# Other weight slots for V, a weighted k without GpSimd, and w_mo loaded within the first tile of an mLSTM core

## The chip, the cores and the metric

The kernel runs on one core of one Trainium2 chip. The metric is the device time of one execution in microseconds (us). A core has five engines: TensorE (PE in the profile; its weight loads are PEld), VectorE (DVE), ScalarE (ACT), GpSimd (POOL) and SyncE (SP), whose queue issues nearly all transfers between DRAM and the on-chip memory SBUF. Matmul results land in PSUM. Each engine works through its own queue in order and waits on semaphores for the others.

## The reference

Two sequences (2048 and 256 tokens, 1024 wide) go through two layers and a final norm:

```python
xn = rms_norm(x, norm_g[0]); x = x + window_attention_mixer(xn, ...)   # 16 heads, 4 KV heads, window 128
xn = rms_norm(x, norm_g[1]); x = x + mlstm_mixer(xn, ...)              # 4 heads, both directions
y  = rms_norm(x, final_norm_g)
```

The change lies in the second layer. It projects `xn` to q, k (512 each), v, o, z (1024 each) and 16 gates. For each head and direction, running over chunks s of the sequence, with weights w made of the gates:

```python
C_loc = einsum('bhcsk,bhcsv->bhckv', w[..., None] * kc, vc)   # state of one chunk
C_new = sp * C + sl * C_loc                                   # carried on
num   = P @ vc + sc * (qc @ C)                                # P: decay times q k^T
h     = num / max(|den|, exp(-m))
```

The two directions are added, normalized, multiplied by `sigmoid(o) * silu(z)` and projected by `w_out` (in the kernel `w_mo`).

## The kernel before

The 2304 tokens are 18 tiles of 128 (`NT`); the kernel takes 128 tokens as one chunk. Every fp32 product is made of three matmuls on parts: a value is split into `hi` (a cast to fp32r) and `lo` (the rest), and hi*hi, lo*hi and hi*lo are added. So each weight block of 128 x 512 that is loaded costs a transfer into a raw buffer, a cast on ACT and a subtraction on DVE. `stage` (line 109) takes the next raw buffer of a ring and issues the transfer on SP (line 113); the ring `raww` has eight buffers (`NRW`).

The parts go into **slots**. `self.free` is a queue of 29: `y0` to `y7`, `w0` to `w15`, `x0` to `x4`, in three pools. `slot` (line 130) takes the first one, `release` (line 179) puts the taken ones back in front, in the order in which they were taken. A slot that is taken again can be written only when the last matmul that read it is done.

The stages in order, each of them a method:

- attention: `attn_core`, `attn_gate`, `attn_out`.
- `mlstm_qkv` (line 640): q and k by `winograd_pass` (line 337), over pairs of tiles. It loads 16 quarter blocks (`quarters`, line 200, the parts by `part`, line 184, with the cast at line 189 and the subtraction at line 190). The first pair is multiplied plainly (`plain`, line 314), and meanwhile `combinations` (line 212) makes the Strassen-Winograd sums `t2`, `t3`, `t1`, `t4` of the quarters (subtractions at lines 218, 226). The other pairs use seven products in the order `b11`, `t2`, `b21`, `t3`, `t1`, `t4`, `b22` (`winograd`, line 277; its half products are lines 273 to 275). 28 slots are in use then, and are released in that order.
- V in the same method: `load_w` (line 138; cast at line 165 or, with a scale, 167; subtraction at line 169 or 171) fills 24 slots with the V columns of `w_qkvg`: eight for the first block of 512, then eight times two for blocks of 272 and 256. Then each tile is projected (`project`, line 371).
- `gate_sums` (line 686): small operations that make the gates' sums and maxima. The scan over the tiles is lines 742 and 745, about 70 operations on DVE; the exponentials on ACT are lines 749, 756, 769, 776.
- `mlstm_gates_states` (line 814): two Winograd passes over `w_oz` (sigmoid at line 851, products at lines 853 and 858, the result `go` stored at line 859) and, between the pairs, the states of the backward direction. `weighted_k` (line 790) makes w*k for one tile: a multiplication on POOL (line 796), a cast on ACT (797), a subtraction on DVE (798), each over all four heads at once. Here it is called with d=1 and a ring of three raw buffers, `rawk`.
- `mlstm_core` (line 865): per tile, four generators: `weights(t+1)` makes the decay matrices and loads the next tile's operands (E at line 887; products at lines 904 to 911), `core(t)` computes the heads, `update(t)` the forward state (it calls `weighted_k` with d=0, and raw buffers of `raww`), `back(t-1)` projects by `w_mo`. The string `ORDER` says how their steps are interleaved. `w_mo`, 16 blocks, is loaded after `weights(0)` and ahead of that loop, into the 16 `w` slots, which the last pass over `w_oz` still uses. `update(t)` runs for all tiles but the last of each sequence, 16 of 18.

The order on each engine isn't the program's order alone. The kernel is built with a scheduler that simulates the engines with estimated times and lays out each queue: what is ready first goes first, and of what is ready, what stands earlier in the program. So work is taken up as early as its buffers are free, sometimes stages ahead, but the order is fixed before the kernel runs.

Of the kernel before, what the change touches and what calls it, by code (L numbers as in the profile page):

```python
# [11 lines left out]
F32 = mybir.dt.float32  # L12
F32R = mybir.dt.float32r
BF16 = mybir.dt.bfloat16
AF = mybir.ActivationFunctionType
ALU = mybir.AluOpType
# [11 lines left out]
MH, DQK, DV = 4, 128, 256  # L28
# [17 lines left out]
AORDER = "fffssssfsffffppsvppv"  # L46
AORDER1 = "fffssssfsffffppsvppv"
AORDER2 = "ssppsspvpv"
KX, WL = 0, 0
PH3, PL3 = (), ()  # L50
EA, ES, EQ = 2, 18, 0
ORDER = "cubwbubccucbcbuwubbbbbbw"
# [3 lines left out]
def seg_of(t):  # L56
    for s in SEGS:
        if s[0] <= t < s[1]:
            return s


class Trunk:
# [577 lines left out]
    def mlstm_qkv(self, first):  # L640
        nc, tc, a = self.nc, self.tc, self.a
        with ExitStack() as st:
            p = st.enter_context(tc.tile_pool(name="b1", bufs=2, reuse_waits="tile"))
            ps = st.enter_context(tc.tile_pool(name="b1ps", bufs=1, space=PSUM, reuse_waits="tile"))
            nc.sync.dma_start(self.gbias, a["gbias"].to_broadcast([128, 16]))

            def use(t, b, o, u):
                y = p.tile([128, MH, DQK], F32, tag="qk"[b], name="qk"[b], bufs=2)
                yf = y[:].rearrange("p h d -> p (h d)")
                if u is None:  # L650
                    nc.scalar.copy(yf, o)
                else:
                    nc.vector.tensor_add(yf, o, u)
                if b:
                    nc.scalar.mul(yf, yf, DQK ** -0.5)
                    nc.sync.dma_start(self.k[t][:], y[:])
                tp = ps.tile([128, MH, 128], F32, tag="tr", name="tr", bufs=1)
                for h in range(MH):
                    nc.tensor.transpose(tp[:, h, :], y[:, h, :], self.ident[:])
                yT = p.tile([128, MH, 128], F32, tag="yT", name="yT", bufs=2)  # L660
                (nc.vector.tensor_copy if b else nc.scalar.copy)(yT[:], tp[:])
                nc.sync.dma_start((self.kT if b else self.qT)[t][:], yT[:])

            self.winograd_pass(self.xn2T, a["w_qkvg"], 0, None, use, first=first)


            w = self.load_w(a["w_qkvg"][:, 1024:], [[512], [272, 256]])
            self.release()
            for t in range(NT):
                xs = self.load_x(self.xn2T[t])  # L670
                v = p.tile([128, MH, VW], F32, tag="v", name="v", bufs=2)
                nc.gpsimd.memset(v[:, :, DV:], 1.0)
                for b in range(3):
                    pj = self.pj()
                    self.project(pj, xs, w[b])
                    if b == 0:
                        nc.scalar.copy(v[:, 1:3, :DV], pj[:].rearrange("p (h d) -> p h d", h=2))
                    elif b == 1:
                        nc.vector.tensor_copy(v[:, 0, :DV], pj[:, :DV])
                        nc.vector.tensor_add(self.gates[:, t, :], pj[:, DV:DV + 16], self.gbias)  # L680
                    else:
                        nc.vector.tensor_copy(v[:, 3, :DV], pj[:, :DV])
                nc.sync.dma_start(self.v[t][:], v[:])
# [106 lines left out]
    def weighted_k(self, p, t, d, raw=()):  # L790

        nc = self.nc
        k = self.stage(self.k[t][:].rearrange("p h d -> p (h d)"), *raw).rearrange("p (h d) -> p h d", h=MH)
        lo = p.tile([128, MH, DQK], F32R, tag="kl", name="kl", bufs=1)
        hi = p.tile([128, MH, DQK], F32R, tag="kh", name="kh", bufs=1)
        nc.gpsimd.tensor_mul(k, k, self.w[:, d, t, :].unsqueeze(2).to_broadcast([128, MH, DQK]))
        nc.scalar.copy(hi[:], k)
        nc.vector.tensor_sub(lo[:], k, hi[:].bitcast(F32))
        return hi, lo
# [65 lines left out]
    def mlstm_core(self, y):  # L865
        nc, tc, a = self.nc, self.tc, self.a
        with ExitStack() as st:
            pool = lambda n, **k: st.enter_context(tc.tile_pool(name=n, bufs=2, reuse_waits="tile", **k))
            TRP, TRT = self.sps, "s"
            py, pv, pm, p, pe = pool("b3y", side="right"), pool("b3v"), pool("b3m"), pool("b3"), self.early  # L870
            ps = pool("b3ps", space=PSUM)
            cm = self.cm
            w = []
            fg = pm.tile([128, D], F32, tag="fg", name="fg", bufs=1)
            nc.sync.dma_start(fg[:], a["final_g"].to_broadcast([128, D]))
            state = {0: None}
# [71 lines left out]
            def update(t):  # L948
                s0, s1 = seg_of(t)
                if t == s1 - 1:  # L950
                    state[t + 1] = None
                    return
                kw = self.weighted_k(pv, t, 0, () if t < KX else ("raww",))
                yield
                C = p.tile([128, MH, VW], F32, tag="C", name="C", bufs=2)
                state[t + 1] = C
                for h in range(MH):
                    self.state_update(ps, 0, t, kw, W[t][3], state[t], C, t == s0, [h], 1)
                    yield

            def back(t):
                hh = H[t][:].rearrange("p h d -> p (h d)")
                xs = []
                for b in range(2):
                    tp = TRP.tile([128, 4, 128], F32, tag=TRT, name="tr", bufs=1)
                    for j in range(4):
                        nc.tensor.transpose(tp[:, j, :], hh[:, (b * 4 + j) * 128:(b * 4 + j + 1) * 128], self.ident[:])
                    xs += self.split(tp[:].rearrange("p c q -> p (c q)"))
                    yield
                x = [p.tile([128, 512], F32, tag="x", name="x", bufs=3)[:] for b in range(2)]  # L970
                for b in range(2):
                    nc.sync.dma_start(x[b], self.x2[t][:, b * 512:(b + 1) * 512])
                for b in range(2):
                    po = self.pj()
                    for qt in range(4):
                        self.project(po, xs, w[b], range(qt * 2, qt * 2 + 2))
                        if qt == 3:
                            nc.vector.tensor_add(x[b], x[b], po[:])
                        yield
                rs = p.tile([128, 1], F32, tag="rs", name="rs", bufs=2)  # L980
                self.rms(p, x, rs[:])
                for b in range(2):
                    cols = slice(b * 512, (b + 1) * 512)
                    nc.vector.scalar_tensor_tensor(x[b], x[b], rs[:], fg[:, cols], ALU.mult, ALU.mult)
                    nc.sync.dma_start(y[t * 128:(t + 1) * 128, cols], x[b])
                yield

            self.free = deque(x for x in self.free if x[0] is self.wp)
            for _ in weights(0):
                pass  # L990
            if not WL:
                w += self.load_w(a["w_mo"], [[512]] * 2, self.g[:, 2], PH3, PL3)
            for t in range(NT + 1):
                gens = {"c": core(t) if t < NT else iter(()), "u": update(t) if t < NT else iter(()),
                        "b": back(t - 1) if t > 0 else iter(()), "w": weights(t + 1) if t + 1 < NT else iter(())}
                for i, k in enumerate(ORDER):
                    if t == 0 and i == WL and WL:
                        w += self.load_w(a["w_mo"], [[512]] * 2, self.g[:, 2], PH3, PL3)
                    next(gens[k], None)
                for g in gens.values():  # L1000
                    for _ in g:
                        pass
# [111 lines left out]
```

## Time and profile before

| | |
|---|---|
| median of three runs | 2317.96 us (2316.12 to 2319.85) |
| profiled execution | 2321.67 us, its span 2319.6 us |
| granted clock of TensorE | 0.98 of full speed on average |
| busy in the span | PE 96%, PEld 76%, DVE 67%, ACT 47%, POOL 20% |

In the stage views each row is a stretch of the span: its limits, its length, then the busy time of PE, PEld, DVE, ACT and POOL with the number of instructions in brackets, the granted clock, the busy share of the DMA engines and GB/s. In a timeline a row is a start, a duration, the engine, the line, the operation, what it writes and reads, and in square brackets how long the engine was idle before and what ended that. "x3" merges three operations that follow each other. In a group the last column is idle time of the engine before these instructions. `ACTq` or `SPq` is the sequencer of an engine.

### The profile page before, as it was taken

How to read it: one execution, taken by the hardware profiler on the slowest of the kernel's cores; microseconds unless marked ns; L12 is line 12 of the kernel's file. 1: busy time of each engine (PE TensorE's matmuls, PEld its weight loads, DVE VectorE, ACT ScalarE, POOL GpSimd, SP SyncE). 2: the span in 40 equal slices, each digit the busy share in tenths (PEclk: the TensorE clock that was granted, in tenths of full speed). 3: DMA queues.
4: the chain of work that ended last, by engine and by line, in shares of the span. 5: the costliest groups of instructions: out<-in, count | busy, mean ns of one | idle time of the engine just before them, and what ended most of it. 6: DMA issues, size and time to landing. Idle time of an engine off the chain costs nothing.

```text
span 2319.6 us, 32951 instructions
## 1 busy us (share of the span) xinstructions
PE 2225.3 (96%) x11102; PEld 1769.0 (76%) x11102; DVE 1549.3 (67%) x3403; ACT 1089.6 (47%) x2500; POOL 456.4 (20%) x392
## 2 busy tenths in 40 slices
PE   8999999999999999999999999969999996999998
PEld 7766666666667887888788899858887885888887
DVE  7565656565877779778656311577698676777784
ACT  6454545454764335445434211454353444554453
POOL 3211111111102221322000000012232216333320
PEclk9999999999999999999999999979999997999999
DMA  7111111111215457667534522443465357655551
GB/s 264 48 38 48 38 48 38 48 41 37 95 53 198 156 166 235 215 204 235 190 121 164 171 97 95 158 160 120 146 211 184 117 186 252 215 191 202 207 164 69
DMA packets 170281, 326.41 MB, mean 141 GB/s; under 512 B 18784, under 2 KB 21632, under 8 KB 170112
## 3 DMA queue, kind: packets, MB, share of 16 engines
q1 hardware_dynamic: 169968, 324.30, 41.8%
q8 instruction: 88, 1.44, 0.3%
q14 instruction: 81, 0.66, 0.1%
q10 hardware_dynamic: 144, 0.01, 0.0%
HBM read 235.34 MB, written 88.89 MB: 140 GB/s over the span
## 4 chain that ended last, share of the span: by engine, by line
PE 71%; DVE 12%; DMA 7%; ACT 6%; issue 3%; POOL 1%; SPq 0%; DVEq 0%; POOLq 0%; ACTq 0%
PE pj L377 8%; PE pj L379 8%; PE pj L378 8%; PE pj L273 4%; PE pj L275 4%; PE pj L274 4%; PE ptp L528 3%; PE o L540 3%; PE c L274 3%; PE c L273 3%; PE c L275 3%; PE d L273 3%; PE d L274 3%; PE d L275 3%; DMA qs<-rows 2%
## 5 line engine op out<-in xcount | busy, mean ns | idle before, releaser
L122 ACT CAST xhi<-rawx 128x512 fp32r<-128x512 f32 x372 | 228.5, 619 | 475.8 <-PE pj L378 106.8
L377 PE MATMUL pj<-whi,xhi 128*128 128x512 f32 (+2 forms) x1152 | 433.2, 377 | 10.1 <-ACT whi L167 5.6
L379 PE MATMUL pj<-whi,xlo 128*128 128x512 f32 (+2 forms) x1152 | 422.6, 372 | 5.2 <-DVE xlo L123 5.2
L378 PE MATMUL pj<-wlo,xhi 128*128 128x512 f32 (+2 forms) x1152 | 425.7, 370 | 0.0
L123 DVE TENSOR_TENSOR xlo<-rawx,xhi 128x512 fp32r<-128x512 f32 x338 | 241.9, 720 | 77.5 <-ACT xhi L122 71.1
L377 PEld LDWEIGHTS pj<-whi,xhi 128*128 128x128 f32 x1152 | 217.5, 189 | 52.1 <-issue 8.8
L379 PEld LDWEIGHTS pj<-whi,xlo 128*128 128x128 f32 x1152 | 217.5, 189 | 49.8 <-DVE xlo L123 9.4
L378 PEld LDWEIGHTS pj<-wlo,xhi 128*128 128x128 f32 x1152 | 217.4, 189 | 36.2 <-issue 2.4
L515 ACT ACTIVATE Sm<-Sm,nm 128x384 f32<-128x384 f32 (+1 forms) x288 | 167.1, 582 | 94.8 <-DVE nm L509 88.4
L273 PE MATMUL pj<-whi,xhi 128*128 128x512 f32 x480 | 196.0, 409 | 5.2 <-ACT xhi L122 1.7
L274 PE MATMUL pj<-wlo,xhi 128*128 128x512 f32 x480 | 194.2, 405 | 1.7 <-DVE wlo L190 1.7
L275 PE MATMUL pj<-whi,xlo 128*128 128x512 f32 x480 | 192.9, 403 | 0.0
L504 DVE CUSTOM_DVE_ANT_0 Sm<-s,mask 128x384 f32<-128x384 f32 (+1 forms) x272 | 136.0, 529 | 71.0 <-PE s L502 67.9
L528 PE MATMUL ptp<-ident,Sm 128*128 128x128 f32 x800 | 135.7, 282 | 8.3 <-DVE PT L531 5.1
L528 PEld LDWEIGHTS ptp<-ident,Sm 128*128 128x128 f32 x800 | 95.6, 142 | 52.2 <-ACT Sm L515 18.0
L274 PE MATMUL d<-wlo,xhi 128*128 128x512 f32 x320 | 126.7, 396 | 1.3 <-DVE wlo L190 1.3
L273 PE MATMUL c<-whi,xhi 128*128 128x512 f32 x320 | 127.6, 399 | 0.0
L274 PE MATMUL c<-wlo,xhi 128*128 128x512 f32 x320 | 127.4, 398 | 0.0
L275 PE MATMUL c<-whi,xlo 128*128 128x512 f32 x320 | 127.2, 398 | 0.0
L273 PE MATMUL d<-whi,xhi 128*128 128x512 f32 x320 | 127.1, 397 | 0.0
L275 PE MATMUL d<-whi,xlo 128*128 128x512 f32 x320 | 126.8, 396 | 0.0
L189 ACT CAST whi<-raww 128x512 fp32r<-128x512 f32 x144 | 86.1, 618 | 76.6 <-DVE raww L218 25.2
(241 smaller groups left out, 4678.8 us busy)
## 6 DMA issues: line engine op xcount, KB each, us to landing
rawx<-xn2T SPq DMA_DIRECT2D x144, 256.0 KB, 3.1
x<-x SPq DMA_DIRECT2D x108, 256.0 KB, 3.9
rawx<-xT SPq DMA_DIRECT2D x72, 256.0 KB, 2.9
raww<-w_oz SPq DMA_DIRECT2D x64, 256.0 KB, 4.3
raww<-w_qkvg SPq DMA_DIRECT2D x40, 256.0 KB, 3.5
v<-v SPq DMA_DIRECT2D x18, 516.0 KB, 3.7
rawx<-v SPq DMA_DIRECT2D x36, 258.0 KB, 2.8
rawx<-x SPq DMA_DIRECT2D x36, 256.0 KB, 3.0
```

The lines of the kernel that those rows point to most:

```text
L122: nc.scalar.copy(hi[:], src)
L123: (eng or nc.vector).tensor_sub(lo[:], src, hi[:].bitcast(F32))
L189: nc.scalar.copy(hi[:], raw)
L273: nc.tensor.matmul(o, xh, wh, start=i == 0 and not more, stop=False, skip_group_check=more)
L274: nc.tensor.matmul(o, xh, wl, start=False, stop=False, skip_group_check=more)
L275: nc.tensor.matmul(o, xl, wh, start=False, stop=i == 3, skip_group_check=more)
L377: nc.tensor.matmul(o[:, :n], xh, wh, start=kt == 0, stop=False)
L378: nc.tensor.matmul(o[:, :n], xh, wl, start=False, stop=False)
L379: nc.tensor.matmul(o[:, :n], xl, wh, start=False, stop=kt == KT - 1)
L504: nc.vector.tensor_tensor_reduce(Sm[:, :nk], S[:, :nk], mask[:, t % 3, win, :], 1.0, MASKED, ALU.add, ALU.max, mx[:, c:c + 1])
L515: nc.scalar.activation(Sg[c][:, :nk], Sg[c][:, :nk], AF.Exp, bias=nm[:, c:c + 1], scale=HD ** -0.5, accum_out=rs[:, c:c + 1])
L528: nc.tensor.transpose(tp[:, c, :], Ss[g][c][:, j, :], self.ident[:])
```

## The change

Three edits. In `mlstm_qkv`, before V's weights are loaded, the queue of free slots is turned so that the slot that the pass over q and k left unused comes first, the five next (the first ones released) are set aside, and V takes the other 24. Afterwards the five come to the front, followed by the others of their pool, so that the pass over `w_oz` takes these first. In `weighted_k`, for d=0 only, the multiplication on POOL is left out: per head, ACT makes `hi` as k times the weight, and DVE makes `lo` as k times the weight less `hi`. Its raw buffers in the core are two that are taken off the ring `raww`, which keeps six. And `w_mo` is loaded inside the loop, at step 12 of the 24 of tile 0, instead of ahead of it.

```diff
-KX, WL = 0, 0
+WL = 12
@@ mlstm_qkv
             self.winograd_pass(self.xn2T, a["w_qkvg"], 0, None, use, first=first)
+            self.free.rotate(1)
+            last = self.free.popleft()
+            kept = [self.free.popleft() for _ in range(5)]
+            self.free.appendleft(last)
             w = self.load_w(a["w_qkvg"][:, 1024:], [[512], [272, 256]])
             self.release()
+            first = [x for x in self.free if x[0] is kept[0][0]]
+            self.free = deque(kept + first + [x for x in self.free if x not in first])
@@ weighted_k
+        if d == 0:
+            for h in range(MH):
+                wk = self.w[:, d, t, h:h + 1]
+                nc.scalar.activation(hi[:, h], k[:, h], AF.Copy, scale=wk)
+                nc.vector.scalar_tensor_tensor(lo[:, h], k[:, h], wk, hi[:, h].bitcast(F32), ALU.mult, ALU.subtract)
+            return hi, lo
         nc.gpsimd.tensor_mul(k, k, self.w[:, d, t, :].unsqueeze(2).to_broadcast([128, MH, DQK]))
         nc.scalar.copy(hi[:], k)
         nc.vector.tensor_sub(lo[:], k, hi[:].bitcast(F32))
@@ mlstm_core
             w = []
+            ring = self.rings["raww"]
+            self.rings["rawk"] = deque(ring.pop() for _ in range(2))
@@ update
-                kw = self.weighted_k(pv, t, 0, () if t < KX else ("raww",))
+                kw = self.weighted_k(pv, t, 0, ("rawk",))
@@ the loop of mlstm_core
-            if not WL:
-                w += self.load_w(a["w_mo"], [[512]] * 2, self.g[:, 2], PH3, PL3)
             for t in range(NT + 1):
...
                 for i, k in enumerate(ORDER):
-                    if t == 0 and i == WL and WL:
+                    if t == 0 and i == WL:
                         w += self.load_w(a["w_mo"], [[512]] * 2, self.g[:, 2], PH3, PL3)
```

## The prediction

> **What bounds the kernel now.** I read the page's busy times first, then the busy times by stage, then the timelines of the stages that the diff touches.
>
> ```profile
> span 2319.6 us, 32951 instructions
> PE 2225.3 (96%) x11102; PEld 1769.0 (76%) x11102; DVE 1549.3 (67%) x3403; ACT 1089.6 (47%) x2500; POOL 456.4 (20%) x392
> ```
>
> TensorE (PE) is busy 96% of the span, so only the 94.3 us in which it stands still, or runs at a low clock, can be won. The next view gives the stages (us; busy time of PE, PEld, DVE, ACT, POOL with instruction counts; granted clock; DMA share; GB/s).
>
> ```profile
> 1255.00:1285.00 30.00, 30.00 (x141) 24.46 (x140) 22.64 (x43) 18.39 (x40) 0.00 (x0) 1.00 0.79 263
> 1440.00:1480.00 40.00, 40.00 (x263) 36.67 (x262) 8.96 (x20) 6.69 (x11) 0.32 (x3) 1.00 0.21 73
> 1491.60:1528.00 36.40, 25.34 (x122) 20.30 (x120) 33.01 (x72) 20.31 (x33) 0.00 (x0) 0.90 0.76 253
> 1528.00:1542.60 14.60, 5.07 (x19) 3.98 (x19) 9.76 (x74) 5.19 (x11) 1.83 (x2) 0.50 0.22 72
> 1911.80:1953.00 41.20, 20.72 (x89) 16.43 (x87) 27.81 (x52) 20.36 (x51) 28.18 (x23) 0.67 0.85 298
> 1953.00:2300.00 347.00, 341.76 (x1884) 293.56 (x1884) 256.57 (x643) 178.27 (x502) 106.19 (x95) 1.00 0.54 180
> ```
>
> V's start (1255 to 1285) and V itself have PE full. Two holes remain beside the diff: the gate sums after V (1491.6 to 1542.6, PE idle 11.1 + 9.5 = 20.6 us) and the start of the core (1911.8 to 1953, idle 20.5 us). The core's later tiles lose 5.2 us in 347. So the forecast is about those two holes.
>
> In the first hole the chain of waits and the timelines show what ends it.
>
> ```profile
> 1515.47 1.05 PE L897 MATMUL s<-qT,kT 128*128 128x128 f32 x8
> ...
> 1542.62 0.79 PE L273 MATMUL pj<-whi,xhi 128*128 128x512 f32 x1 [1.61 <-DVE e L853]
> ```
>
> ```profile
> 1533.89 0.32 ACT L749 ACTIVATE spr<-spr 1x144 f32<-1x144 f32 x1 [7.72 <-DVE spr L748]
> ...
> 1541.25 1.08 ACT L851 ACTIVATE e<-pj 128x512 f32<-128x512 f32 x2
> ```
>
> PE waits for a PSUM buffer that the sigmoid of line 851 has to read; on ACT that sigmoid stands behind the exponentials of the gate sums, and the first of these waits 7.72 us for DVE. DVE is 33.01 of 36.4 us busy until 1528, then runs the scan alone. So DVE's load ahead of the scan sets when PE goes on.
>
> **The change part by part. 1: other slots for V.** Followed through the queue of free slots by hand: before, V takes the slots y0 to y7 for its first block, and the first eight of the 16 quarter blocks of w_oz need just those, so their casts wait for V's last tile. After, V takes x4 (unused until now), y5 to y7, and slots of `b21`, `t3`, `t1`, `t4` and `b22`; y0 to y4 stay free.
>
> ```profile
> L113 SPq DMA_DIRECT2D raww<-w_oz x8: 328/382/390, 1274.8 to 1284.1; - x8
> ```
>
> ```profile
> 1481.48 4.82 ACT L189 CAST whi<-raww 128x512 fp32r<-128x512 f32 x7 [0.20 <-PE pj L379]
> ```
>
> ```profile
> 1482.32 4.70 DVE L190 TENSOR_TENSOR wlo<-raww,whi 128x512 fp32r<-128x512 f32 x7
> ```
>
> ```profile
> 1483.04 11.91 SPq L113 DMA_DIRECT2D raww<-w_oz  x14
> ```
>
> The loads are issued as early as their raw buffers allow (1274.8), 200 us before their casts. With five slots free I expect five casts and five subtractions to go up into V's stage, where DVE has 31 of 40 us free, and five of the 14 loads now issued from 1483 on to follow them. The hole then loses 5 x 4.70/7 = 3.4 us of DVE work, and perhaps DVE's waits for those loads:
>
> ```profile
> L190 DVE TENSOR_TENSOR wlo<-raww,whi 128x512 fp32r<-128x512 f32 x32 | 21.2, 684 | 1.6 <-ACT whi L189 1.6
> L226 DVE TENSOR_TENSOR raww<-raww 128x512 f32<-128x512 f32 x4 | 2.7, 685 | 2.8 <-DMA raww<-w_oz 2.8
> ```
>
> 2.8 us at line 226. Both ends: -6.2 us, and +2 us if the queue of DVE is laid out anew with the gate steps later (three 0.67 us operations put ahead of them; no row excludes it). I take **-4.5**: all of the work, and 1.1 of the 2.8, since most loads stay. The half clock after the pause (0.50 until 1542.6) stays, because 16 us of pause remain.
>
> ```profile
> 1953.54 0.23 PE pj L378
> ```
>
> The price is at V's start: the last four blocks of V's weights now wait for `b22`, which the last pair of q and k uses last. PE has no idle time there (30.00 of 30.00), and behind that product lie V's first block and six of eight steps of its second as other work: 24 matmuls at 0.23 us (a step of the chain, from a later stage) are 5.6 us, against a cast and a subtraction of 4.82/7 + 4.70/7 = 1.4 us for the first. I take 0; with that cover gone it is +2.8 us for four narrower blocks of half that cost each.
>
> **2: weighted k without GpSimd (POOL).** Per tile this removes one multiplication on POOL, one 512-wide cast on ACT and one 512-wide subtraction on DVE; it adds four 128-wide scaled copies on ACT and four fused operations on DVE.
>
> ```profile
> L796 POOL TENSOR_TENSOR raww<-raww,scr x16: 1034/1038/1484, 1918.9 to 2080.6; 128x512 f32<-128x512 f32 x16
> L798 DVE TENSOR_TENSOR kl<-raww,kh x16: 679/1255/1840, 1922.5 to 2245.0; 128x512 fp32r<-128x512 f32 x16
> L797 ACT CAST kh<-raww x16: 602/610/631, 1920.4 to 2244.4; 128x512 fp32r<-128x512 f32 x16
> L906 ACT ACTIVATE E<-E,scr x144: 384/390/405, 1545.6 to 2248.4; 128x128 f32<-128x128 f32 x144
> L931 DVE SCALAR_TENSOR_TENSOR r<-num,scr x72: 143/150/160, 1923.1 to 2288.0; 128x2 f32<-128x2 f32 x72
> L935 DVE SCALAR_TENSOR_TENSOR hh<-num,r,hh x72: 470/480/486, 1927.6 to 2290.9; 128x256 f32<-128x256 f32 x72
> ```
>
> ACT: 4 x 0.39 for 0.61, at most +0.95 us a tile. DVE: a fused operation of width 128 lies between 0.15 (width 2) and 0.48 (width 256); halfway, 0.31, gives 1.26 for four, against 0.68 undisturbed and 1.26 in the median. In the later tiles this lies under PE (DVE 74%, ACT 51% busy of 347 us), and I cost it at nothing; with the cover gone it is 16 x 0.58 = 9.3 us.
>
> [...]
>
> **3: k's own two buffers, and w_mo later.** This is about the second hole, on SP's queue and POOL:
>
> ```profile
> 1920.92 2.00 SPq L113 DMA_DIRECT2D raww<-k  x2
> 1923.22 0.32 SPq L859 DMA_DIRECT2D go<-e  x1
> ```
>
> ```profile
> 1918.86 1.48 POOL L796 TENSOR_TENSOR raww<-raww,scr 128x512 f32<-128x512 f32 x1
> 1920.31 1.72 POOL L858 TENSOR_TENSOR e<-e 128x512 f32<-128x512 f32 x1
> ...
> 1925.48 8.02 POOL L796 TENSOR_TENSOR raww<-raww,scr 128x512 f32<-128x512 f32 x8
> ```
>
> ```profile
> 1918.93 0.63 ACT L851 ACTIVATE e<-s 128x512 f32<-128x512 f32 x1 [1.07 <-POOL e L858]
> ```
>
> ```profile
> go<-e SPq DMA_DIRECT2D x36, 256.0 KB, 3.2
> ```
>
> ```profile
> 1923.22 5.17 DMA go<-e
> ...
> 1929.78 5.74 DMA E<-rows
> ...
> 1935.55 1.04 DVE E L904
> ```
>
> With eight raw buffers k is loaded many tiles ahead, just where the last gate product `go` has to be stored; its store is ahead of E of tile 1 on SP's queue, and E starts the chain to 1953. Without line 796 the last `e` is ready at 1918.93 + 0.63 + 1.72 = 1921.3 instead of 1922.0, and without the two k loads its store is issued then, not at 1923.22: -1.9 us. The store takes 5.17 us against a median of 3.2; six fewer k loads (256 KB each, 1.6 MB) and two more of w_mo (its ring has six buffers now) leave 1.05 MB less to move, 3.5 us at the stage's 298 GB/s, if all of that were waited for. Against it stands k's cast on the same chain, +0.6 to +1.2. Ends: -1.9 - 3.5 = -5.4, and +1.2 without any gain; I take **-3.0**.
>
> All 16 loads of w_mo, with 16 ACT and 16 DVE operations, are moved behind half of tile 0 in the program. In the trace before:
>
> ```profile
> 1914.65 7.92 DVE L171 SCALAR_TENSOR_TENSOR wlo<-raww,g,whi 128x512 fp32r<-128x512 f32 x5
> ```
>
> ```profile
> 1953.04 0.50 PE L377 MATMUL pj<-whi,xhi 128*128 128x512 f32 x1 [0.57 <-ACT xhi L122]
> ```
>
> they end at 1922.6 and are first read at 1953.04: 30 us of slack, so I cost the move at nothing.
>
> Sum: -4.5 - 3.0 + 0 = -7.5 us. The profiled execution took 2321.67 us (span 2319.6 and 2.1 around it), 3.7 over the median of 2317.96; I subtract from the median: **2310.5 us**.
>
> **The rivals.** *Only one hole shrinks* (the gate chain keeps its place among DVE's work, or E's load still waits): -3 to -4.5, about 2314. For it: both are orders laid out from estimated times. *Nothing changes*, 2318: the five casts aren't taken up into V, because the free slots are no use while the raw buffers hold others; the eight early loads at 1274.8 speak against it. *w_mo comes late* (the slower one): casts left over at 1922.6 run into the chain of 1935 to 1953.
>
> ```profile
> 1920.00:1930.00 10.00, 4.20 (x13) 3.29 (x14) 4.58 (x11) 6.68 (x18) 9.37 (x9) 0.50 0.76 277
> 1930.00:1940.00 10.00, 3.73 (x24) 3.00 (x22) 4.19 (x12) 4.14 (x14) 6.00 (x6) 0.84 1.02 346
> 1940.00:1953.00 13.00, 9.48 (x36) 8.01 (x36) 10.84 (x22) 4.05 (x11) 7.16 (x6) 0.57 0.69 239
> ```
>
> DVE has 5.4 + 5.8 + 2.2 = 13.4 us free there, room for eight casts at the 7.92/5 = 1.58 us just shown. From the ninth on each costs 1.58; all 16 cost 12, less 4.5 from the first hole: +7.5, 2325.5. *POOL's relief helps the core*: of its 106 us of POOL work 16 x 1.04 = 16.6 go, and DVE's 1.26 against 0.68 at line 798 tells of disturbance. Then the core's 5.2 us of PE idle time go too: -12.7, 2305. [...]
>
> **How the numbers follow.** Forecast 0.48; one hole 0.20; nothing 0.12; w_mo late 0.13; POOL's relief 0.07. A measurement of this kernel can't tell less than about 0.2%, 4.6 us, from no change. Faster: most of the forecast (0.43), the relief (0.07), a third of one hole (0.07): 0.57. Slower: w_mo late and a little of nothing: 0.15. Same: 0.28. The forecast's own ends are -6.2 - 5.4 = -11.6 and about -3; with the relief -16.8, 2301, and with a small loss 2321. Outside lies most of w_mo late and little else.
>
> **What would show it.** Five of line 189's casts between 1285 and 1480, and 27 instead of 32 of line 190 in the first hole; the scan (lines 742, 745) starting some 4 us sooner after V's last tile; no run of k loads ahead of the last `go` store, E of tile 1 landing about 3 us sooner; line 171 ended before DVE starts on E. I am wrong if V's start gets PE idle time, if casts of line 171 stand between E's arrival and the first line 377, or if the scan starts as late as before.

## The result, and the profile after

The changed kernel takes 2322.18 us (median of 13 runs, 2320.42 to 2324.25); the kernel before, run beside it, 2316.77 us (13 runs, 2311.99 to 2319.85). The ratio is 1.0026, 95% interval 1.0017 to 1.0035: slower by 4 to 8 us, where 7.5 us less had been forecast. The time lies just above the forecast's range, which ended at 2321.

The page of the changed kernel (span; busy time of each engine, share of the span, instructions):

```profile
span 2321.4 us, 33033 instructions
PE 2221.7 (96%) x11102; PEld 1763.0 (76%) x11102; DVE 1548.0 (67%) x3451; ACT 1099.5 (47%) x2548; POOL 436.8 (19%) x376
```

The profiled execution took 2323.22 us, 1.0 over its median, while that of before stood 4.9 over its own. So spans can't be set against each other directly. Five events that both programs have cut the execution into stretches. First their rows in the timeline of the changed kernel (start, duration, engine, line, operation; in brackets the idle time before it and what ended that): a step of the normalization on POOL, V's last matmul, the first product that the hole of the gate sums holds up, and the first projection of the core.

```profile
1041.42 0.55 POOL L391 TENSOR_TENSOR rs<-ss,epst 128x1 f32<-128x1 f32 x1 [6.12 <-DVE ss L390]
...
1497.85 0.28 PE L379 MATMUL pj<-whi,xlo 128*128 128x256 f32 x1
...
1546.29 0.79 PE L273 MATMUL pj<-whi,xhi 128*128 128x512 f32 x1 [1.61 <-DVE e L865]
...
1949.85 0.50 PE L377 MATMUL pj<-whi,xhi 128*128 128x512 f32 x1 [0.68 <-ACT xhi L122]
```

The first two in the timeline of the kernel before (the other two, at 1542.62 and 1953.04, stand in the prediction), with its two copies of q, which matter below:

```profile
1044.12 0.55 POOL L391 TENSOR_TENSOR rs<-ss,epst 128x1 f32<-128x1 f32 x1 [6.23 <-DVE ss L390]
...
1098.57 0.56 ACT L651 COPY q<-pj 128x512 f32<-128x512 f32 x1
...
1102.61 0.57 ACT L651 COPY q<-pj 128x512 f32<-128x512 f32 x1
...
1492.09 0.28 PE L379 MATMUL pj<-whi,xlo 128*128 128x256 f32 x1
```

Before, this first event is 2.7 us later, in a part of the program that the change doesn't touch; a stretch that begins there is free of that. The lengths in us:

| | to V's last matmul | the hole | to the first projection | to the end | all four |
|---|---|---|---|---|---|
| before | 448.3 | 50.3 | 410.4 | 366.6 | 1275.5 |
| after | 456.7 | 48.2 | 403.6 | 371.6 | 1280.0 |
| difference | +8.5 | -2.1 | -6.9 | +5.0 | +4.5 |

So the second half wins 4.0 us, and everything is lost ahead of V's end, where nothing had been forecast. The stages of the changed kernel (limits, length, busy time of PE, PEld, DVE, ACT, POOL, granted clock, DMA share, GB/s):

```profile
1044.00:1145.00 101.00, 94.36 (x432) 76.83 (x431) 78.30 (x135) 54.21 (x103) 14.71 (x13) 0.97 0.69 226
1115.00:1120.00 5.00, 5.00 (x14) 3.85 (x14) 3.56 (x12) 3.55 (x7) 0.00 (x0) 0.59 0.92 279
1276.00:1300.00 24.00, 21.67 (x119) 18.36 (x118) 15.56 (x33) 12.81 (x29) 0.00 (x0) 1.00 0.84 286
1498.10:1546.30 48.20, 29.67 (x135) 23.47 (x133) 40.55 (x142) 23.55 (x40) 1.64 (x2) 0.78 0.59 190
1908.80:1949.80 41.00, 24.62 (x115) 19.27 (x113) 31.94 (x61) 25.25 (x62) 14.75 (x11) 0.83 0.84 298
1949.80:2321.40 371.60, 354.84 (x1939) 303.23 (x1939) 270.29 (x701) 190.91 (x553) 100.34 (x92) 0.99 0.54 177
```

The same view of the kernel before, where the prediction doesn't have it:

```profile
1044.00:1145.00 101.00, 99.20 (x459) 80.41 (x458) 80.16 (x137) 56.94 (x110) 15.08 (x12) 0.98 0.69 226
1276.00:1300.00 24.00, 24.00 (x139) 20.79 (x138) 13.01 (x27) 9.73 (x21) 0.00 (x0) 1.00 0.79 268
1953.00:2319.60 366.60, 353.64 (x1936) 302.92 (x1936) 262.92 (x655) 181.51 (x510) 107.31 (x97) 1.00 0.52 174
```

PE stands still for 6.6 us in 1044 to 1145 (before 1.8) and 2.3 us at V's start (before nothing). The 6.6 us are one wait. In the timeline of the changed kernel the transposes of q (line 659) wait for the copies of q on ACT (line 651):

```profile
1112.20 0.62 ACT L165 CAST whi<-raww 128x512 fp32r<-128x512 f32 x1 [1.74 <-DMA raww<-w_qkvg]
...
1113.24 1.06 ACT L651 COPY q<-pj 128x512 f32<-128x512 f32 x2
...
1113.88 1.11 PE L659 MATMUL tr<-ident,q 128*128 128x128 f32 x4 [6.64 <-ACT q L651]
```

Before, the copies ran at 1098.57 and 1102.61; now both run at 1113.24. Two things stand ahead of them that hadn't: the rest of the attention stage's work, and the cast of V's first weight block (line 165), which waits 1.74 us for its load. The wait at V's start is the same kind of thing on the same queue:

```profile
1285.32 0.62 ACT L189 CAST whi<-raww 128x512 fp32r<-128x512 f32 x1 [3.20 <-DMA raww<-w_oz]
...
1287.00 0.62 ACT L189 CAST whi<-raww 128x512 fp32r<-128x512 f32 x1
...
1287.90 0.62 ACT L189 CAST whi<-raww 128x512 fp32r<-128x512 f32 x1
...
1292.32 0.62 ACT L189 CAST whi<-raww 128x512 fp32r<-128x512 f32 x1 [1.54 <-DMA raww<-w_oz]
...
1296.35 0.62 ACT L189 CAST whi<-raww 128x512 fp32r<-128x512 f32 x1 [2.45 <-DMA raww<-w_oz]
1296.88 1.04 ACT L165 CAST whi<-raww 128x272 fp32r<-128x272 f32 x3
...
1297.35 0.39 PE L377 MATMUL pj<-whi,xhi 128*128 128x272 f32 x1 [2.31 <-ACT whi L165]
```

These are the five casts of w_oz that were to go up into V's stage. The last of them waits 2.45 us for its load, and V's last casts stand behind it.

Why should a slot move the copies of q? In the built program the fifth x slot, `x4`, which no stage used before, has no memory until something takes it. V's first block now does. The pool of the x slots grows by the slot's 4096 bytes, and the pools stacked behind it move down (bytes of a partition):

```
                                  before            after
x slots (right side)          180192-196576     176096-196576
split and raw buffers         159520-180192     155424-176096
attn_out's own tiles          141984-159520     137888-155424
mlstm_qkv's tiles (left)      118624-139168     118624-139168
```

Before, 2816 bytes lay between the last two; now they share 1280. The shared bytes belong to a buffer of `v` and to one of `attn_out`'s `x`; q's own buffers (118624-122720) touch none of `attn_out`'s, before or after. Why the copies of q are put behind the end of that stage all the same isn't shown here; the runs below show that they are. Hence the first theory, **placement**: the work of `mlstm_qkv` is laid behind the end of the attention stage, because their tiles share addresses. The rival is the **early cast**: the cast of V's first block, taken up ahead of the copies of q, holds them up.

### The profile page after: what moved, and what is told of

Its sections match the earlier page's. It is cut to its first block, busy times and chain, and to the rows that moved or that the text cites. A ratio compares the mean times of both kernels' runs of the same rounds, so it can differ in the third digit from the quotient of the medians.

```text
span 2321.4 us, 33033 instructions
## 1 busy us (share of the span) xinstructions
PE 2221.7 (96%) x11102; PEld 1763.0 (76%) x11102; DVE 1548.0 (67%) x3451; ACT 1099.5 (47%) x2548; POOL 436.8 (19%) x376
```

## The experiments: the start of the q/k pass

All ratios are against the kernel before, with 95% intervals.

**Memory alone.** The kernel before with 4 KB more behind the x slots:

```diff
                 self.free.extend((wx, f"x{i}") for i in range(NWX))
+                nc.gpsimd.memset(wx.tile([128, 2, 512], F32, tag="pad", name="pad", bufs=1)[:, :, :1], 0.0)
```

> The kernel before with nothing changed but 4 KB per partition more in the pool of the x slots, of which one column is written and nothing is read: as much as the fifth x slot takes when it is used for the first time. The pools behind it move down by 4096 bytes, and the pool of the last attention stage then overlaps that of the q, k, v stage by 1280 bytes (before there were 2816 bytes between them). Theory 'placement': the q copies at the start of the q/k pass are laid behind the end of the attention stage, TensorE stands still for some 5 us there, and the time is about 2316.8 + 5 = 2322 us (2320 to 2324). Rival 'early cast' (the cast of V's first weight block, which was hoisted ahead of the q copies, holds them up on ACT): no such cast is hoisted here, so the time stays at 2317 us (2315 to 2318.5).

Measured: 2318.94 us, ratio 1.0017 (1.0008 to 1.0026), +3.9 us. Of its waits (what waited for what: total, times, longest), its stages and its timeline:

```profile
PE tr L659 <- ACT q L651: 3.9, 1, 3.9
```

```profile
1044.00:1145.00 101.00, 96.00 (x443) 77.97 (x442) 79.71 (x136) 53.12 (x101) 14.39 (x12) 0.98 0.68 223
```

```profile
1107.89 1.07 ACT L651 COPY q<-pj 128x512 f32<-128x512 f32 x2
```

The stall is there without any other slot, cast or k: 5.0 us of PE idle against 1.8, and both copies of q run together, behind the attention stage. Placement is shown as a cause. It isn't all: the wait is 3.9 us, not 6.6. The other 2.7 us fit the cast that stands ahead of the copies in the changed kernel and waits 1.74 us; that part is argued.

**The gap opened again**, at the cost of one raw buffer of the backward states:

```diff
-                self.rings["rawk"] = self.slots(self.mid, "rawk", 3)
+                self.rings["rawk"] = self.slots(self.mid, "rawk", 2)
```

> The changed kernel with the ring of the backward states' raw k buffers cut from three to two, so that the attention pool and the q, k, v pool no longer overlap (832 bytes between them). The fifth x slot is still V's first slot, and its cast still goes up among the q copies. Placement: the stall at the start of the q/k pass is gone, 2322.2 - 5 = 2317 us (2315 to 2319), less if the gain of the gate sums is then seen in full, more if the states suffer from the missing buffer. Early cast: the stall stays, 2322 us.

Measured: 2323.48 us, ratio 1.0029 (1.0018 to 1.0041). By the time alone the rival would have won. The trace says otherwise:

```profile
1044.00:1145.00 101.00, 98.27 (x460) 79.30 (x459) 82.11 (x140) 55.59 (x107) 14.55 (x11) 1.00 0.70 233
```

The stall is gone (2.7 us of idle, the clock 1.00), as is the wait at V's start (0.3 us). The stretch to V's last matmul is 449.3 us, 7.4 less than in the changed kernel. But from the hole to the first projection it takes 409.7 us against 403.6, and to the end 782.4 against 775.1, so what the gap won is lost again behind the hole. A part of that lies where the buffer is missing: in the stage of the backward states PE stands still for 7.3 us where it stood 4.8. The rest wasn't traced. The edit wasn't neutral; a cleaner one follows below.

**Four slots kept back**, so that `x4` stays unused:

```diff
-            self.free.rotate(1)
-            last = self.free.popleft()
-            kept = [self.free.popleft() for _ in range(5)]
-            self.free.appendleft(last)
+            kept = [self.free.popleft() for _ in range(4)]
```

> The changed kernel with four slots kept back in place of five; V takes the other 24 of the 28 used ones, and the fifth x slot stays unused, so no address moves. Placement: no stall at the start of the q/k pass, four casts of w_oz instead of five go up into V's stage, the hole of the gate sums shrinks by about 3.5 us; with the 2.3 us of waiting at V's start left, 2322.2 - 5 to - 7 = 2315 to 2317 us, PE idle from 1044 to 1255 us about 2 us as in the kernel before. Early cast: 2317 us as well (no cast goes up), so this run is for the size of the rest.

> The slots' part of the change alone, with four slots kept back as in the run with four, on the kernel before (k through GpSimd, w_mo ahead of the loop). If the k and w_mo parts win 3 us at the core's start, as predicted, this is 3 us slower than the run with four slots kept back and all three parts: 2318 to 2320 us; if those two parts win nothing, the two are equal within 1 us.

Measured: with all three parts 2314.41 us, ratio 0.9987 (0.9978 to 0.9997); the slots' part alone 2316.26 us, 1.0006 (0.9997 to 1.0015). PE idles 1.1 us in 1044 to 1145 in the first. The two differ by 0.0019, by their intervals some 1 to 7 us: with four slots the k and w_mo parts are worth about the 3 us that had been forecast (2.3 by their traces, in the last table of the next section), the slots alone nothing that can be told from zero.

**The change without the overlap.** `x4` gets a pool of its own, opened when the attention stage's pool is closed:

```diff
                     first = self.attn_out(self.attn_gate())
+                late = right("wx4")
+                self.free = deque((late if x[1] == "x4" else x[0], x[1]) for x in self.free)
```

> The changed kernel, with five slots kept back, where the fifth x slot gets a pool of its own that is opened behind the attention stage, so that the attention pool stays where it was before and doesn't overlap that of q, k and v. Everything else is the change. Placement: the stall at the start of the q/k pass is gone (PE idle from 1044 to 1145 us at most 2 us, in place of 6.6, and no clock of 0.59 behind it), and the wait at V's start with it, as in the two earlier runs without the overlap: 2322.2 - 7 = 2315 us (2313 to 2317). Rival (the stall only hides a loss that the queue meets anyway, at V's start or in the hole of the gate sums): 2319 to 2322 us.

Measured: 2311.62 us, ratio 0.9981 (0.9972 to 0.9990). Its stage and its timeline:

```profile
1044.00:1145.00 101.00, 100.06 (x469) 81.14 (x468) 83.37 (x143) 57.64 (x109) 14.58 (x11) 1.00 0.71 234
```

```profile
1096.22 0.56 ACT L651 COPY q<-pj 128x512 f32<-128x512 f32 x1
...
1100.26 0.56 ACT L651 COPY q<-pj 128x512 f32<-128x512 f32 x1
...
1117.47 0.62 ACT L165 CAST whi<-raww 128x512 fp32r<-128x512 f32 x1 [0.91 <-DMA xn2T<-xo]
```

Everything else of the change is there, and it is 4.4 us faster than before instead of 6 us slower. The copies of q are back in their place, with the early cast behind them; at V's start PE idles 0.6 us of 45 in place of 2.3. The address of one slot was worth 10 us (1.0026 against 0.9981). What this run doesn't separate is the cast from the overlap: once the overlap goes, the cast isn't ahead of the copies either.

## The experiments: k, its buffers and w_mo

After the first projection the changed kernel gives back 5.0 of the 6.9 us that it won on the way there. Theory **narrow operations**: the four fused operations of line 806 put more on DVE than costed. Its row in the changed kernel (duration in ns, minimum, median and maximum), and what goes on around one group of them:

```profile
L806 DVE SCALAR_TENSOR_TENSOR kl<-rawk,scr,kh x64: 323/345/1385, 1902.4 to 2250.0; 128x128 fp32r<-128x128 f32 x64
```

```profile
L806 DVE SCALAR_TENSOR_TENSOR kl<-rawk,scr,kh 128x128 fp32r<-128x128 f32 x64 | 40.5, 663 | 0.0
```

```profile
1941.19 3.19 DVE L806 SCALAR_TENSOR_TENSOR kl<-rawk,scr,kh 128x128 fp32r<-128x128 f32 x4
...
1941.49 2.73 POOL L925 TENSOR_TENSOR qs<-qT,qs 128x512 f32<-128x512 f32 x2 [5.87 <-issue]
```

The median is 0.345 us, near the 0.31 that was estimated, but the mean is 0.663: while POOL works (1941.49 to 1944.22), four take 3.19 us. In all that is 40.5 us on DVE in place of 19.7, the subtractions of the kernel before:

```profile
L798 DVE TENSOR_TENSOR kl<-raww,kh 128x512 fp32r<-128x512 f32 x16 | 19.7, 1229 | 0.2 <-ACT kh L797 0.2
```

Rivals: the loss belongs to **w_mo's move**; or the win is **given back** whatever k does, since the later tiles are paced by something else.

**k alone, and w_mo alone.** The first as a diff against the changed kernel, the second against the kernel before:

```diff
-            self.free.rotate(1)
-            last = self.free.popleft()
-            kept = [self.free.popleft() for _ in range(5)]
-            self.free.appendleft(last)
...
-            first = [x for x in self.free if x[0] is kept[0][0]]
-            self.free = deque(kept + first + [x for x in self.free if x not in first])
...
+            w += self.load_w(a["w_mo"], [[512]] * 2, self.g[:, 2], PH3, PL3)
             for t in range(NT + 1):
...
-                    if t == 0 and i == WL:
-                        w += self.load_w(a["w_mo"], [[512]] * 2, self.g[:, 2], PH3, PL3)
```

```diff
-KX, WL = 0, 0
+KX, WL = 0, 12
```

> The k part alone (weighted k on ACT and DVE, two raw buffers of its own; V's slots and w_mo as in the kernel before). Theory 'narrow operations': the four fused operations of 0.66 us each per tile put 20.8 us more on DVE, PE waits longer for the projection's splits (lines 122 and 123) after the core's start, and from the core's first projection to the end it takes 4 to 5 us more than the 366.6 us before; the core's start itself is some us shorter, since no burst of k products stands on POOL there: 2316.8 - 4 + 4.5, about 2317 us (2314 to 2319). Rival 'w_mo': the loss in the later tiles belongs to w_mo's move, so this run has only the gain, 2312 to 2314 us.

> w_mo's move alone (step 12 of tile 0; V's slots and k as in the kernel before). Narrow operations: no loss in the later tiles, at most a small gain at the core's start: 2315 to 2317 us. Rival 'w_mo': from the core's first projection to the end 4 to 5 us more than 366.6, and 2318 to 2321 us.

Measured: k alone 2325.47 us, ratio 1.0035 (1.0023 to 1.0046), more than either theory gave; w_mo alone 2318.80 us, 1.0011 (1.0002 to 1.0020). With k alone the stretch after the first projection is 379.2 us, 12.6 longer than before. One place in its windows and its timeline:

```profile
2242.00:2262.00 20.00, 17.70 (x81) 14.89 (x82) 13.37 (x32) 10.37 (x29) 3.75 (x4) 0.83 0.23 70
```

```profile
2240.25 3.18 POOL L912 TENSOR_TENSOR E<-E,cm 128x512 f32<-128x512 f32 x2 [2.67 <-DMA E<-rows]
...
2240.95 2.63 DVE L800 SCALAR_TENSOR_TENSOR kl<-rawk,scr,kh 128x128 fp32r<-128x128 f32 x2
```

Two of the narrow operations take 2.63 us under POOL's product of E, the split of a projection comes behind them, PE waits 2.9 us for it and then runs at half its clock (0.50) until 2250:

```profile
2244.30 0.80 PE L379 MATMUL pj<-whi,xlo 128*128 128x512 f32 x1 [2.95 <-DVE xlo L123]
```

```profile
2246.00:2250.00 4.00, 4.00 (x10) 3.06 (x10) 0.86 (x2) 1.13 (x5) 0.00 (x0) 0.50 0.01 4
```

That is a few us of the 12.6; the rest was not traced to a place.

**The new k for the first tile alone**, and for none, both with four slots kept back, k's own buffers and w_mo moved:

```diff
-        if d == 0:
+        if d == 0 and t == 0:
```

```diff
-        if d == 0:
+        if d < 0:
```

> All three parts with four slots kept back, but the new weighted k for the first tile alone; the other 15 tiles have the multiplication on POOL, one cast and one subtraction again, from the two buffers of k's own. Narrow operations: the core's start is as short as with all three parts and the later tiles are as before, 2314.4 - 4 = 2310.5 us (2308 to 2312.5). Rival 'given back' (the tiles behind the start are paced by something else, and what is won at the start is lost there whatever k does): 2314 us.

> The same with POOL's multiplication for all 16 tiles: only the two buffers and w_mo's move are left of those two parts. If the core's start was won by the absence of the burst (eight k products at once on POOL ahead of E), this equals the run with the new k in the first tile alone, about 2310.5 us; if it was won by POOL's multiplication being gone, the start is as long as before and the time is 2314 to 2316 us.

Measured: 2310.97 us, ratio 0.9972 (0.9961 to 0.9984), and 2316.77 us, 0.9997 (0.9989 to 1.0006). By these times it is the new k in the first tile that wins, and not the absence of the burst of k products on POOL: with POOL's product everywhere nothing is left. That goes against the reason that the prediction gave, too, since without the burst the run of k loads ahead of `go`'s store is gone as well. The traces show a smaller difference than the times: 1.6 us from the first event to the end (the table below), where the medians differ by 5.8. How the new k in one tile wins was not traced.

Three more with the new k in the first tile alone: the first has five slots and the late pool, the other two are the kernel with 2310.97 us, one with w_mo ahead of the loop again, one with V's slots as before.

```diff
                 late = right("wx4")
...
-        if d == 0:
+        if d == 0 and t == 0:
```

```diff
+            w += self.load_w(a["w_mo"], [[512]] * 2, self.g[:, 2], PH3, PL3)
             for t in range(NT + 1):
...
-                    if t == 0 and i == WL:
-                        w += self.load_w(a["w_mo"], [[512]] * 2, self.g[:, 2], PH3, PL3)
```

```diff
-            kept = [self.free.popleft() for _ in range(4)]
...
-            first = [x for x in self.free if x[0] is kept[0][0]]
-            self.free = deque(kept + first + [x for x in self.free if x not in first])
```

> The same with the new weighted k for the first tile alone. Narrow operations: lower than the run before this by 3 to 4 us, as 2311.0 was lower than 2314.4 with four slots: 2311 to 2312 us. Given back: equal to the run before this within 1.5 us.

> Four slots kept back, the new weighted k for the first tile alone, k's own buffers, and w_mo loaded ahead of the loop as in the kernel before. If w_mo's move costs in itself what it cost alone (2318.8 against 2316.25, +2.5 us): 2308.5 us. If the move is worth something once the burst of k products is gone (its 16 casts and subtractions then stand where E is late): 2312 to 2314 us.

> The new weighted k for the first tile alone, k's own buffers and w_mo's move, with V's slots as in the kernel before. If keeping four slots back is worth what the shorter hole of the gate sums shows (0.2 to 0.5 us of its length): 2311 to 2312 us. If it is worth the predicted 3.5 us: 2314.5 us.

Measured: 2311.36 us, ratio 0.9981 (0.9971 to 0.9991); 2311.94 us, 0.9973 (0.9963 to 0.9983); 2310.15 us, 0.9976 (0.9967 to 0.9984). All are faster than both kernels, and none differs from the others by more than the intervals.

The stretches of all runs, in us and worked out as above, show what single times can't:

| | to V's last matmul | the hole | from the hole to the end | all, against before |
|---|---|---|---|---|
| before | 448.3 | 50.3 | 777.0 | |
| after | 456.7 | 48.2 | 775.1 | +4.5 |
| memory alone | 451.4 | 50.5 | 777.1 | +3.5 |
| gap, two raw buffers | 449.3 | 48.7 | 782.4 | +5.0 |
| four slots, all parts | 447.3 | 50.0 | 774.8 | -3.3 |
| four slots alone | 447.8 | 49.7 | 777.0 | -1.0 |
| k alone | 448.3 | 50.9 | 784.4 | +8.1 |
| w_mo alone | 448.3 | 50.3 | 777.0 | +0.1 |
| four slots, first tile | 447.2 | 48.6 | 775.4 | -4.3 |
| four slots, POOL's k | 446.4 | 49.8 | 776.6 | -2.6 |
| five slots, late pool | 447.2 | 47.8 | 776.7 | -3.8 |
| the same, first tile | 447.0 | 48.9 | 774.0 | -5.6 |
| first tile, w_mo ahead | 446.9 | 49.5 | 772.2 | -7.0 |
| first tile, V's slots as before | 448.3 | 50.1 | 773.6 | -3.5 |

Rows of programs that agree in a stretch agree to 0.1 us there: 448.3 in the four kernels with V's slots and all addresses as before, 777.0 to 777.1 behind the hole in the four with POOL's k and `raww` (the kernel before, memory alone, four slots alone, w_mo alone). Where two executions differ all the same, it can be ahead of the first event: the profiled one of w_mo alone is 4.1 us shorter than that of the kernel before (2317.56 against 2321.67), and its first event is 4.1 us earlier (1040.04 against 1044.12).

The first projection, on the other hand, is no event at which kernels can be compared. Those four reach it 410.4, 409.6, 407.5 and 406.4 us behind the hole, and POOL's k with its own buffers 402.2; what came sooner there is gone again at the end, with the old k as well. So the 5.0 us above don't speak for narrow operations. The rival "given back" holds for that stretch, and only the time to the end counts.

Behind the hole the four kernels with the new k in the first tile alone take 773.8 us on average, 3.2 less than the kernel before; the three with it in every tile and w_mo moved 774.8 to 776.7 (the one with two raw buffers is left out). On average narrow operations in every tile would cost some 1.7 us of those 3.2. But the two pairs that differ in this alone disagree: with five slots every tile takes 2.6 us more than the first alone (776.7 against 774.0), with four 0.6 less (774.8 against 775.4), and the times show no difference in the first pair (2311.62 against 2311.36) and 3.4 us more in the second (2314.41 against 2310.97). So a cost of the narrow operations isn't shown with w_mo moved. Why k alone, with w_mo ahead of the loop, takes 784.4 stays open.

## Why the prediction was wrong, step by step

**The step that failed** is half a sentence: "V takes x4 (unused until now)". It was costed at nothing, as one slot like another. It was the first use of a slot, so it needed memory, the memory moved a neighbour, and the neighbour's overlap moved work of a stage that the diff doesn't touch: +8.5 us to V's last matmul. The memory alone, in the kernel before, makes 3.1 of them (451.4 against 448.3); the rest came with the overlap and the early casts together, 2.3 of it at V's start. Nothing in the list of rivals was near it; "w_mo comes late" had the sign and another place.

With the slot put where it moves nothing, the time is 2311.62 us where 2310.5 was forecast. That is near in part by luck. Against the kernel before beside it this run is 4.4 us faster by the ratio and 3.8 by the traces, not 7.5. Of the 3.8 the hole gives 2.4 where 4.5 were forecast, the time behind the hole 0.3 where 3.0 were, and 1.1 come ahead of V's end, where nothing was. So both terms of the sum were too large as well, for the reasons below.

**First hole, -4.5.** The mechanism was right, and the size was off by half. Five casts of line 189 went up (1285.32 to 1296.35). In the timelines, from the last copies beside V's gates (line 679, then 685) to the first operation behind the scan (748, then 754); in the changed kernel:

```profile
1498.29 0.42 DVE L685 COPY v<-pj 128x256 f32<-128x256 f32 x1
...
1537.23 0.29 DVE L754 TENSOR_TENSOR spr<-rw 1x144 f32<-1x144 f32 x1
```

and before:

```profile
1490.26 0.42 DVE L679 COPY v<-pj 128x256 f32<-128x256 f32 x1
...
1533.56 0.30 DVE L748 TENSOR_TENSOR spr<-rw 1x144 f32<-1x144 f32 x1
```

From the one to the other 43.3 us before, 38.9 after: 4.4 less, as forecast. But the hole of PE shrank by 2.1 only. The copy came 1.8 us ahead of V's last matmul before (1490.26 against 1492.09) and comes 0.4 us behind it now (1498.29 against 1497.85): DVE reaches V's last gates 2.3 us later. Ten subtractions of line 190 stand right ahead of that copy in both kernels, though five of the 32 had gone up, as forecast (from 1482 to 1546 us there are 27): the five next took their places. In the changed kernel they wait 2.9 us for their casts, before 1.3, and one of line 226 stands there too (0.6 us more). The sum counted the work that left the chain, not what was put ahead of the chain's first link. With five slots the hole is 47.8 to 48.9 us, without any 50.1 to 50.9.

**V's start, 0, or +2.8 with the cover gone.** The prediction named idle time of PE here as a sign of being wrong, and it came: 2.3 us in the changed kernel. In the runs without the overlap that have the early casts (two raw buffers, four slots, the late pool), no wait there is longer than 0.3. (The cover of 24 matmuls at 0.23 us is 5.5 us, not 5.6, which changes nothing.) Neither the cover nor the late slots did it: a cast of w_oz that was taken up early stood ahead of V's casts and waited for its own load. That goes with the overlap; the kernel with the memory alone, which has no early casts, doesn't have it.

**k on ACT and DVE, 0, or +9.3 with the cover gone.** The price of one operation was right undisturbed (0.345 against 0.31), and twice that on average. PE's longest sum of waits from 1955 us on, before and then in the changed kernel, is that for the projection's `xlo`, which DVE makes:

```profile
PE pj L379 <- DVE xlo L123: 5.2, 7, 1.3
```

```profile
PE pj L379 <- DVE xlo L123: 7.5, 9, 1.5
```

The cover held in part: this wait grew by 2.3 us.

**Second hole, -3.0.** The signs that were named came true in the changed kernel. On SP's queue, and in the chain of waits:

```profile
1922.11 3.32 SPq L871 DMA_DIRECT2D go<-e  x2
...
1929.51 0.38 SPq L901 DMA_DIRECT2D E<-rows  x1
```

```profile
1925.10 2.98 DMA go<-e
...
1929.51 5.93 DMA E<-rows
```

No run of k loads stands ahead of the last store of `go`, which takes 2.98 us where it took 5.17, and E lands at 1935.44. Counted from the first product behind the hole that is 389.2 us, against 392.9 before (1935.52 less 1542.62): 3.7 sooner, where 3 were forecast. PE idles 16.4 us in the 41 us ahead of the first projection, against 20.5. By the end 1.9 us of that stayed (775.1 against 777.0), and 0.3 in the run without the overlap.

What failed is the step's premise, that an earlier E is won at the end. With w_mo's move alone, POOL's products and the run of k loads are all still there, and DVE starts on E as soon behind the hole as in the changed kernel (1927.78 less 1538.61, 389.2 us):

```profile
1927.78 1.72 DVE L904 TENSOR_TENSOR E<-E,cm 128x512 f32<-128x512 f32 x2 [3.55 <-DMA E<-rows]
```

Yet from the hole to the end that kernel takes the same 777.0 us as the one before. With POOL's product kept, but without the burst, DVE starts on E 387.3 us behind the hole (1927.02 less 1539.77), 5.7 sooner than before, and 776.6 of 777.0 us are left. And where DVE starts on E 388.1 and 388.8 us behind the hole (the new k in the first tile with w_mo ahead of the loop, and k alone), the times to the end are 772.2 and 784.4. So E's arrival, which the sum priced, doesn't decide the end by itself; what does stays open.

**w_mo moved, 0.** Alone it is +2.5 us (1.0011, 1.0002 to 1.0020), by the trace +0.1; the extra time isn't found in its trace. Beside the new k in the first tile the times show no difference (0.9973 without the move, 0.9972 with it), while by the traces the kernel without it is 2.7 us shorter (-7.0 against -4.3). The slack held as it was read: line 171 ends at 1930.6 us in the changed kernel, 19 us ahead of the first projection. But two casts of w_mo (line 167, at 1920.64 and 1921.32) now stand in the chain that leads to `go`'s last store.

## What to carry to other kernels

A buffer, slot or tile that was declared but never used is not free: its first use takes memory (here 4096 bytes of a partition) and can slide stacked pools into an overlap (here of 1280 bytes). Before a change is costed, compare the addresses of neighbouring stages, and look at the order of work there as well as at the lines of the diff. And a gain is to be followed to an event that no kernel can move: here 4 us at the chain became 2 us of PE's hole, and 7 us on the way to the first projection became 2 us at the end. Whether a chain sets the end shows in a kernel that shortens it alone: E came 3.8 us sooner with w_mo's move alone, and the time from the hole to the end stayed the same.

## What the hardware showed

The same fused DVE operation of 128 columns takes 0.323 to 0.347 us in the 34 of 64 cases in which no POOL product runs beside it, and up to 1.385 us beside one; four of them took 3.19 us over a POOL span of 2.73. The 26 that began while a POOL product ran all end 0.15 to 0.17 us behind the end of one, however early they began. One of them in the timeline of the changed kernel (POOL ends at 2185.04, the operation at 2185.19):

```profile
2182.49 2.55 POOL L918 TENSOR_TENSOR E<-E,cm 128x512 f32<-128x512 f32 x2 [2.25 <-DMA E<-rows]
...
2184.01 1.18 DVE L806 SCALAR_TENSOR_TENSOR kl<-rawk,scr,kh 128x128 fp32r<-128x128 f32 x1
```

So the narrow operation is not slowed in proportion here: it ends 0.15 us after the POOL operation has ended, and takes 1.18 us where it takes 0.345 in the median. By what means the one holds up the other isn't shown.

PE's pause of 6.64 us was followed by a clock of 0.59 over 5 us (1115 to 1120); behind that of 2.31 us at V's start it was 1.00 (1297.3 to 1305). Behind the pause of 2.95 us in the run with k alone it was 0.50 over 4 us (2246 to 2250). So in these runs a pause of 2.95 us was followed by half the clock and one of 2.31 us by the full one; what decides it isn't shown.
